# The grouped-query projection ahead of the first scores, and a bias table stored in reverse

## The chip, the cores and the metric

The kernel runs on one core of a Trainium2 chip. The metric is the device time of one execution in microseconds (us). The kernel before takes 1292.56 us, the median of three runs (1289.69 to 1295.23).

The engines are TensorE (PE: matmuls and transposes; PEld is its weight load), VectorE (DVE), ScalarE (ACT), GpSimd (POOL) and SyncE (SP), whose queue issues nearly all transfers.

## The reference

Two post-norm layers on 512 tokens of width 1024. Each layer projects x once, gives the columns to three kinds of attention, joins the heads by one output projection, and ends in a SwiGLU feed-forward part.

```python
for l in range(DEPTH):                       # DEPTH = 2, B = 1, S = 512
    h = x @ w_in[l]                          # 1024 -> 2080 columns
    # A, columns 0 to 415: latent attention (q rank 256, kv rank 128, rotary key 32), 6 heads
    cq, ckv = rms_norm(h[..., :256], mla_q_norm[l]), rms_norm(h[..., 256:384], mla_kv_norm[l])
    ...
    out_a = dense_attention(qa, ka, va, 96 ** -0.5)
    # B, columns 416 to 1567: dilated windows (128,1), (512,4), (2048,16), 6 heads, relative bias
    out_b = dilated_mixture(hb[:, :, 0], hb[:, :, 1], hb[:, :, 2], rel_bias)
    # C, columns 1568 to 2079: grouped-query attention, 4 query and 2 key-value heads
    qc, kc = rms_norm(qc, gqa_q_norm[l]), rms_norm(kc, gqa_k_norm[l])
    qc, kc = (concat([rope(a[..., :32], row_pos), rope(a[..., 32:], col_pos)]) for a in (qc, kc))
    out_c = dense_attention(qc, kc, vc, 64 ** -0.5)
    x = layer_norm(ALPHA * x + concat([out_a, out_b, out_c]) @ w_out[l], ln1_g[l], ln1_b[l])
    ff = (silu(x @ w_gate[l]) * (x @ w_up[l])) @ w_down[l]
    x = layer_norm(ALPHA * x + ff, ln2_g[l], ln2_b[l])
```

All of it is fp32.

## The kernel before

**Precision.** A float32 product is made of three matmuls on split operands: high by high, high by low, low by high (`mm3`, lines 165 to 167). So every weight block is loaded into a staging buffer (`wraw`, line 150, a ring of two), its high part is cast on ScalarE (`whi`, line 152) and its low part subtracted on VectorE or GpSimd (`wlo`, line 156); the table `LOE` names the engine for each kind of weight.

**A layer's projections.** `token_proj` projects columns to tokens: four blocks of 128 tokens (t), each summed over eight blocks of 128 inputs. It serves the value columns of B (96 matmuls of 384 columns, evacuated by `evac_v` into `dv`, line 366), the columns of C (96 matmuls of 512 columns, called the grouped projection here) and the columns of A (96 of 416). `dil_qk(pair)` projects queries and keys of two heads of B (48 matmuls of 512 columns, `qkp`); a pair's keys are copied to the other half of the partitions by transfers (`dk`, line 565). `evac_g2` finishes a token block of the grouped projection: copy, split of the values (`gv`), squares on ScalarE, their sum on VectorE (line 426), the power for the root mean square on GpSimd (line 192), two scalings on VectorE (429, 430, the second by the gain table `gg`), four rotary products on GpSimd (436) and three more operations on VectorE (439 to 446).

**Scores.** `attend` walks over 64 units per layer; a unit is one head's scores for 128 queries: 24 of B, then 16 of C, then 24 of A. Method `a` makes the scores (`sc`, line 241) and the softmax numerators; for B a reduction on VectorE (line 247) adds the bias tile `dt` and finds the extreme in one instruction. Three units later `b` transposes the probabilities (`ptr`, line 264) and splits them (271, 272), and one unit later `c` multiplies them by the values (`po`, 282 and 283).

**Fillers.** Other work is woven between the units as generators: the remaining pairs, the grouped projection, the columns of A, the latents, and the first half of the output projection (`opp`, five of eight blocks). The table `W` gives each filler the first and the last unit between which its steps are spread; `pre` places its weight loads. Before the first unit stand only the value projection, the bias tables and pair zero.

**Order.** Every engine runs its own queue in order. The code's order is the start; the framework's scheduler, which estimates when operands are ready, decides how instructions from neighbouring steps stand against each other in each queue. Within SyncE's queue a transfer waits for those ahead of it to be issued.

**Bias tables (layer 0 only).** `bias_tables` builds a 6 x 1024 table of bias by distance (`nl`: a one-hot matmul `pb` added to the window counts, line 379). Query p of a unit needs the table shifted by p. The table is written to DRAM (`tdr`, 24 KB), spread there to 128 rows of 1025 numbers per head (`skew`, line 385: six transfers of 512 KB) and read back with a row length of 1024, so that each partition starts one number further on (`load_dt`, line 636, 128 x 896). Its matmul takes a bank of the same ring (`ps_mm`) as the value projection and pair zero.

**Gain table.** One buffer `gg` holds C's norm gains of a layer; the loads of layer 1's gains (line 410) reuse it, and VectorE scales them (line 411).

Of the kernel before, what the change touches and what calls it, by code (L numbers as in the profile page):

```python
# [10 lines left out]
F32 = mybir.dt.float32  # L11
# [5 lines left out]
P = 128  # L17
T = 512
# [11 lines left out]
MLA_SCALE = 96.0 ** -0.5  # L30
BRANCHES = ((128, 1), (512, 4), (2048, 16))
NMIX, LA, LC = 13, 3, 1
W = dict(qk1=(3, 4), g2a=(1, 18), qk2=(9, 16), g2b=(10, 16), gT0=(24, 25), gT1=(25, 26), g1=(14, 23), lat=(24, 38),
         lqv=(32, 40), mT=(36, 39, 42, 47, 53, 55), op=(51, 65), tl=69, fl=76, p=(0, 5, 16, 13, 25, 57))
LOE = dict(dl='v', g2='g', op='v', f='g', qk='v', G='g', L='v', uq='v', kv='v', opp='g', rt='g')
QKR = 'wwm'
LEAD = 2
NU = (68, 75)
SPLIT = True
# [3 lines left out]
C_Q, C_K, C_V, C_G = 416, 800, 1184, 1568  # L43
# [13 lines left out]
def _constants():  # L57
    t = np.arange(T)
    rc, rs = _rope_tab(t // GRID_W, HD // 2)
    cc, cs = _rope_tab(t % GRID_W, HD // 2)  # L60
    mc, ms = _rope_tab(t, 32)
    tabs = np.concatenate(
        [np.eye(P), _tok(np.concatenate([rc, cc], 1)), _tok(np.concatenate([rs, cs], 1)), _tok(mc), _tok(ms)], 1
    ).astype(np.float32)
    d = np.arange(-T, T)
    n = np.abs(d)
    nb = BUCKETS // 2
    ex = nb // 2
    nf = np.maximum(n, 1).astype(np.float32)
    large = ex + (np.log(nf / np.float32(ex)) / np.float32(math.log(MAX_DIST / ex)) * np.float32(nb - ex)).astype(np.int32)  # L70
    bucket = np.where(d > 0, nb, 0) + np.where(n < ex, n, np.minimum(large, nb - 1))
    onehot = np.zeros((BUCKETS, 2 * T), np.float32)
    onehot[bucket, np.arange(2 * T)] = -1.0
    cnt = np.zeros(2 * T, np.int64)
    for window, dil in BRANCHES:
        cnt += (d % dil == 0) & (n // dil <= window // (2 * dil))
    neg = np.where(cnt > 0, -np.log(np.maximum(cnt, 1)), 1e30).astype(np.float32)
    return tabs, onehot, neg[None, :]


@with_exitstack
def encoder(ctx: ExitStack, tc, x, w_in, mla_q_norm, mla_kv_norm, w_uq, w_ukv, gqa_q_norm, gqa_k_norm, rel_bias,
            w_out, ln1_g, ln1_b, w_gate, w_up, w_down, ln2_g, ln2_b, tabs, onehot, neglnc, out):
    nc = tc.nc
    V, A, G, TE = nc.vector, nc.scalar, nc.gpsimd, nc.tensor
# [145 lines left out]
    class Head:  # L231
# [4 lines left out]
        def a(self, qt):  # L236

            sc = bank(ps_sc, "sc")
            ops = self.qk(qt)
            for i, (a, b) in enumerate(ops):  # L240
                TE.matmul(sc, a, b, start=i == 0, stop=i == len(ops) - 1)  # L241
            pl = ppl.tile([P, T], F32, tag="l", name="pl")
            nm = small(1, "nm")
            src = sc
            if self.dtile is not None:
                o = 384 - P * qt
                V.tensor_tensor_reduce(out=pl, in0=sc, in1=self.dtile()[:, o:o + T], scale=1.0, scalar=3e38,
                                       op0=ALU.add, op1=ALU.min, accum_out=nm)
                src = pl
            else:  # L250
                V.tensor_reduce(nm, sc, axis=AX.X, op=ALU.min)
            s = small(1, "ssum")
            A.activation(pl, src, AF.Exp, bias=nm, scale=-1.0, accum_out=s)
            r = small(1, "srec")
            V.reciprocal(r, s)  # L255
            G.tensor_tensor(pl, pl, r.to_broadcast([P, T]), op=ALU.mult)  # L256
            self.pl[qt] = pl
# [101 lines left out]
    def run(gen):  # L359
        for _ in gen:  # L360
            pass
# [6 lines left out]
    def bias_tables():  # L368
# [9 lines left out]
            TE.matmul(pb[:6, :], rb, oh[:, i * 512:(i + 1) * 512], start=True, stop=True)  # L378
            V.tensor_tensor(nl[:, i * 512:(i + 1) * 512], nl[:, i * 512:(i + 1) * 512], pb[:6, :], op=ALU.add)
        tdr = dr.tile([6, 2 * T], F32, tag="tdr", name="tdr")  # L380
        nc.sync.dma_start(tdr, nl)

        skew = dr.tile([6, P, 2 * T + 1], F32, tag="skew", name="skew")
        for h in range(6):
            nc.sync.dma_start(skew[h, :, 0:2 * T], tdr[h:h + 1, :].to_broadcast([P, 2 * T]))
        return skew


    skew = []
# [7 lines left out]
    for l in range(DEPTH):  # L397
# [234 lines left out]

        def load_dt(h):
            dt = pdt.tile([P, 896], F32, tag="d", name="dt")
            src = skew[0][h].rearrange("p c -> (p c)")[P:P + P * 2 * T].rearrange("(p c) -> p c", p=P)
            nc.sync.dma_start(dt, src[:, :896])
            dts[h] = dt
            yield

# [39 lines left out]
        if l:  # L679
            run(token_proj(xT, l, C_V, C_G, evac_v, LO["g2"], LATE, ws0))  # L680
        else:
            run(token_proj(xT, l, C_V, C_G, evac_v, V, STAIR, ws0, [ps_mm, ps_mm, ps_sc, ps_sc]))
            skew.append(bias_tables())
        run(dil_qk(0))
        run(load_dt(0))
        run(load_dt(1))
        g2_steps = token_proj(xT, l, C_G, 2080, evac_g2, LO['G'])
        qk = [dil_qk(1), dil_qk(2)]
        g1_steps = token_proj(xT, l, 0, C_Q, evac_g1, LO['L'])
        lqv, op = latent_qv(), out_part()  # L690

        def pre(g, k):
            return (g, 1, W['p'][k], W['p'][k] + 1)

        fillers = [pre(qk[0], 0), (qk[0], 8, *W['qk1']), pre(g2_steps, 1), (g2_steps, 8, *W['g2a']),
                   pre(qk[1], 2), (qk[1], 8, *W['qk2']), (g2_steps, 8, *W['g2b']),
                   (gqa_T(0), 2, *W['gT0']), (gqa_T(1), 2, *W['gT1']), pre(g1_steps, 3), (g1_steps, 16, *W['g1']),
                   (latents(), 4, *W['lat']), pre(lqv, 4), (lqv, 12, *W['lqv'])]
        fillers += [(load_dt(h), 1, 4 * h - 2, 4 * h - 1) for h in range(2, 6)]
# [161 lines left out]
```

## Time and profile before

| what | value |
|---|---|
| median of three runs | 1292.56 us |
| the profiled execution | 1289.81 us |
| its span in the trace | 1288.0 us |
| mean granted TensorE clock | 0.992 |
| TensorE busy | 1252.6 us (97%) |
| six skew writes | 512 KB each |

The span runs from the first to the last recorded instruction; the execution's own time is 1.8 us longer. A granted clock of 1.0 is TensorE at 2.4 GHz, 0.5 at 1.2 GHz; a mean between them is a mixture. The busy time of TensorE is high by nature in this kernel, so the rows to look for are those in which TensorE waits, and the stretches in which another engine sets its pace.

### The profile page before, as it was taken

The page shows a single profiled execution, that of the slowest core. Times are in us where ns is not written, and L with a number is a line of the kernel's source. Part 1 is how long each engine was busy: PE and PEld are TensorE (multiplying, and loading weights), DVE is VectorE, ACT ScalarE, POOL GpSimd, SP SyncE. Part 2 cuts the span into 40 slices and gives each one's busy share as a digit, 9 for nine tenths or more (in the row PEclk, how much of TensorE's full clock was granted, in tenths as well). Part 3 has the DMA queues.
Part 4 walks back from the last instruction along what each step waited for, and adds up shares of the span by engine and source line. Part 5 has one row for each costly group of instructions (what it writes and reads, how often), then busy time and mean ns, then how long its engine had stood idle before and what let it go on. Part 6 is the DMA issues. An engine that isn't in the chain of part 4 may idle for free.

```text
span 1288.0 us, 16749 instructions
## 1 busy us (share of the span) xinstructions
PE 1252.6 (97%) x6352; PEld 1065.2 (83%) x6352; DVE 688.0 (53%) x1138; ACT 543.1 (42%) x955; POOL 323.2 (25%) x344
## 2 busy tenths in 40 slices
PE   8799899999999999999999999999999999999997
PEld 7689788879888888888898898888988888888885
DVE  4259798686333233333564789976843333333346
ACT  3256697554222212222245668865342221122222
POOL 0165474563000000000154456645600000000004
PEclk9999899999999999999999999999999999999999
DMA  5752310323333333333426231105243332333232
GB/s 178 204 137 79 99 40 13 102 83 110 103 96 94 94 96 97 98 98 99 144 80 163 70 99 51 38 14 147 82 114 99 98 98 89 108 96 96 92 100 108
DMA packets 141416, 125.72 MB, mean 98 GB/s; under 512 B 7020, under 2 KB 114668, under 8 KB 141336
## 3 DMA queue, kind: packets, MB, share of 16 engines
q1 hardware_dynamic: 141336, 124.66, 33.1%
q8 instruction: 50, 0.82, 0.3%
q14 instruction: 30, 0.25, 0.1%
HBM read 117.80 MB, written 5.27 MB: 96 GB/s over the span
## 4 chain that ended last, share of the span: by engine, by line
PE 84%; DVE 6%; DMA 4%; ACT 3%; POOL 2%; issue 1%; DVEq 0%; SPq 0%; POOLq 0%; ACTq 0%
PE down L167 6%; PE gate L165 6%; PE down L165 6%; PE up L167 6%; PE up L165 6%; PE down L166 6%; PE gate L167 6%; PE up L166 6%; PE gate L166 6%; PE sc L241 4%; PE ptr L264 3%; PE tp L165 2%; PE tp L166 2%; PE tp L167 2%; PE po L283 2%; PE po L282 2%
## 5 line engine op out<-in xcount | busy, mean ns | idle before, releaser
L152 ACT CAST whi<-wraw 128x1024 fp32r<-128x1024 f32 (+3 forms) x202 | 205.7, 1020 | 553.5 <-PE gate L166 141.8
L156 DVE TENSOR_TENSOR wlo<-wraw,whi 128x1024 fp32r<-128x1024 f32 (+3 forms) x170 | 208.9, 1230 | 319.2 <-ACT whi L152 315.0
L191 POOL TENSOR_TENSOR rstd<-mv,eps_l 128x1 f32<-128x1 f32 x16 | 5.7, 357 | 680.0 <-DVE mv L200 680.0
L256 POOL TENSOR_TENSOR pl<-pl,srec 128x512 f32<-128x512 f32 x128 | 134.2, 1049 | 148.9 <-DVE srec L255 137.4
L166 PE MATMUL gate<-xTl,whi 128*128 128x512 f32 (+1 forms) x384 | 142.9, 372 | 0.0
L166 PE MATMUL up<-xTl,whi 128*128 128x512 f32 (+1 forms) x384 | 142.9, 372 | 0.0
L167 PE MATMUL gate<-xTh,wlo 128*128 128x512 f32 (+1 forms) x384 | 142.8, 372 | 0.0
L167 PE MATMUL up<-xTh,wlo 128*128 128x512 f32 (+1 forms) x384 | 142.8, 372 | 0.0
L165 PE MATMUL up<-xTh,whi 128*128 128x512 f32 (+1 forms) x384 | 142.8, 372 | 0.0
L165 PE MATMUL gate<-xTh,whi 128*128 128x512 f32 (+1 forms) x384 | 142.5, 372 | 0.0
L167 PE MATMUL down<-whi,act 128*128 128x512 f32 x352 | 136.8, 390 | 0.0
L165 PE MATMUL down<-whi,act 128*128 128x512 f32 x352 | 136.8, 390 | 0.0
L166 PE MATMUL down<-wlo,act 128*128 128x512 f32 x352 | 136.8, 390 | 0.0
L156 POOL TENSOR_TENSOR wlo<-wraw,whi 128x512 fp32r<-128x512 f32 (+2 forms) x64 | 79.4, 1263 | 93.4 <-ACT whi L152 72.9
L775 DVE TENSOR_TENSOR sg<-sg,up 128x512 f32<-128x512 f32 x44 | 30.2, 687 | 135.1 <-PE up L167 133.7
L272 DVE TENSOR_TENSOR PTl<-ptr,PTh 128x512 fp32r<-128x512 f32 x128 | 87.2, 682 | 7.8 <-ACT PTh L271 6.8
L271 ACT CAST PTh<-ptr 128x512 fp32r<-128x512 f32 x128 | 75.0, 586 | 38.0 <-PE ptr L264 37.4
L167 PEld LDWEIGHTS gate<-xTh,wlo 128*128 128x128 f32 x384 | 72.4, 189 | 12.5
L166 PEld LDWEIGHTS up<-xTl,whi 128*128 128x128 f32 x384 | 72.4, 189 | 12.5
L165 PEld LDWEIGHTS up<-xTh,whi 128*128 128x128 f32 x384 | 72.4, 188 | 12.5
L167 PEld LDWEIGHTS up<-xTh,wlo 128*128 128x128 f32 x384 | 72.3, 188 | 12.4
L166 PEld LDWEIGHTS gate<-xTl,whi 128*128 128x128 f32 x384 | 72.3, 188 | 12.5
(174 smaller groups left out, 2499.1 us busy)
## 6 DMA issues: line engine op xcount, KB each, us to landing
wraw<-in_ffn_w_down SPq DMA_DIRECT2D x54, 512.0 KB, 3.7
wraw<-in_ffn_w_up SPq DMA_DIRECT2D x44, 512.0 KB, 3.9
wraw<-in_ffn_w_gate SPq DMA_DIRECT2D x44, 512.0 KB, 4.0
wraw<-in_w_in SPq DMA_DIRECT2D x20, 512.0 KB, 4.5
wraw<-in_w_out SPq DMA_DIRECT2D x14, 512.0 KB, 4.0
dt<-skew SPq DMA_DIRECT2D x12, 448.0 KB, 3.2
wraw<-in_w_in SPq DMA_DIRECT2D x8, 416.0 KB, 3.3
wraw<-in_w_in SPq DMA_DIRECT2D x8, 384.0 KB, 3.7
```

What stands on the lines that cost most here:

```text
L152: A.copy(h[:, :n], r[:, :n])
L156: lo.tensor_tensor(o[:, c:c + step], r[:, c:c + step], h[:, c:c + step].bitcast(F32), op=ALU.subtract)
L165: TE.matmul(ps, ah, bh, start=first, stop=False)
L166: TE.matmul(ps, ah, bl, start=False, stop=False)
L167: TE.matmul(ps, al, bh, start=False, stop=last)
L241: TE.matmul(sc, a, b, start=i == 0, stop=i == len(ops) - 1)
L256: G.tensor_tensor(pl, pl, r.to_broadcast([P, T]), op=ALU.mult)
L264: TE.transpose(pb[:, kt * P:(kt + 1) * P], pl[:, kt * P:(kt + 1) * P], ident)
L271: A.copy(ph[:, :, c:c + P], pb)
L272: V.tensor_tensor(plo[:, :, c:c + P], pb, ph[:, :, c:c + P].bitcast(F32), op=ALU.subtract)
L282: TE.matmul(po[:, h0:h0 + 256], self.vst(kt), ph[:, kt], start=kt == 0, stop=False)
L775: V.tensor_tensor(sg, sg, pss[1], op=ALU.mult)
```

## The change

Three edits. The bias table is stored in reverse, so a partition's row is a stretch of the 24 KB table that starts p numbers further on; it is read straight from `tdr` with overlapping rows, `skew` and its six writes go, and the reduction on line 247 reads its tile backwards. The write of `tdr` moves from SyncE's queue to ScalarE's. The grouped projection with its evacuations moves ahead of the first unit in both layers: pair zero's loads, the bias tables (layer 0), the grouped weights' loads, pair zero's matmuls, two bias tiles, then the whole grouped projection. Its low parts move from GpSimd to VectorE (`G`), pair zero's split weights move to the ring `pmix` (`QKR`), and the other fillers get new places in `W`.

```diff
-W = dict(qk1=(3, 4), g2a=(1, 18), qk2=(9, 16), g2b=(10, 16), gT0=(24, 25), gT1=(25, 26), g1=(14, 23), lat=(24, 38),
...
+W = dict(qk1=(1, 7), qk2=(8, 15), gT0=(20, 22), gT1=(28, 30), g1=(13, 25), lat=(25, 30),
...
-LOE = dict(dl='v', g2='g', op='v', f='g', qk='v', G='g', L='v', uq='v', kv='v', opp='g', rt='g')
-QKR = 'wwm'
+LOE = dict(dl='v', g2='g', op='v', f='g', qk='v', G='v', L='v', uq='v', kv='v', opp='g', rt='g')
+QKR = 'mwm'
...
-    onehot[bucket, np.arange(2 * T)] = -1.0
+    onehot[bucket, np.arange(2 * T)[::-1]] = -1.0
...
-    return tabs, onehot, neg[None, :]
+    return tabs, onehot, np.ascontiguousarray(neg[None, ::-1])
...
-                o = 384 - P * qt
-                V.tensor_tensor_reduce(out=pl, in0=sc, in1=self.dtile()[:, o:o + T], scale=1.0, scalar=3e38,
+                o = 895 - (384 - P * qt)
+                V.tensor_tensor_reduce(out=pl, in0=sc, in1=self.dtile()[:, slice(o, o - T if o >= T else None, -1)], scale=1.0, scalar=3e38,
                                        op0=ALU.add, op1=ALU.min, accum_out=nm)
...
         tdr = dr.tile([6, 2 * T], F32, tag="tdr", name="tdr")
-        nc.sync.dma_start(tdr, nl)
-
-        skew = dr.tile([6, P, 2 * T + 1], F32, tag="skew", name="skew")
-        for h in range(6):
-            nc.sync.dma_start(skew[h, :, 0:2 * T], tdr[h:h + 1, :].to_broadcast([P, 2 * T]))
-        return skew
+        A.dma_start(tdr, nl)
+        return tdr
...
-            src = skew[0][h].rearrange("p c -> (p c)")[P:P + P * 2 * T].rearrange("(p c) -> p c", p=P)
-            nc.sync.dma_start(dt, src[:, :896])
+
+            row = skew[0][h:h + 1, :]
+            nc.sync.dma_start(dt, bass.AP(row.tensor, row.offset, [[1, P], [1, 896]]))
...
+        qk = [dil_qk(i) for i in range(3)]
+        g2_steps = token_proj(xT, l, C_G, 2080, evac_g2, LO['G'])
+        next(qk[0])
+        if l == 0:
             skew.append(bias_tables())
-        run(dil_qk(0))
+        next(g2_steps)
+        run(qk[0])
         run(load_dt(0))
         run(load_dt(1))
-        g2_steps = token_proj(xT, l, C_G, 2080, evac_g2, LO['G'])
-        qk = [dil_qk(1), dil_qk(2)]
+
+        run(g2_steps)
...
-        fillers = [pre(qk[0], 0), (qk[0], 8, *W['qk1']), pre(g2_steps, 1), (g2_steps, 8, *W['g2a']),
-                   pre(qk[1], 2), (qk[1], 8, *W['qk2']), (g2_steps, 8, *W['g2b']),
+        fillers = [pre(qk[1], 0), (qk[1], 8, *W['qk1']), pre(qk[2], 2), (qk[2], 8, *W['qk2']),
```

The change moves instructions on all queues; three places follow, each in the order before and then in the changed one. A row is one instruction or a run of like ones: its line, its kind, what it writes and reads, its shape.

SyncE's queue in layer 0, from the bias table's inputs (`nl`) to the first copies of pair zero's keys (`dk`), before:

```order
L375 DMA nl<-in_neglnc 6x1024
L150 DMA wraw<-in_w_in 128x8x128 x4
L381 DMA tdr<-nl 6x1024
L385 DMA skew<-tdr 128x1024 x6
L636 DMA dt<-skew 128x896 x2
L150 DMA wraw<-in_w_in 128x2x512 x2
L565 DMA dk<-dk 64x1024 x2
```

And in the changed kernel:

```order
L375 DMA nl<-in_neglnc 6x1024
L150 DMA wraw<-in_w_in 128x8x128 x2
L150 DMA wraw<-in_w_in 128x2x512 x4
L633 DMA dt<-tdr 128x896 x2
L150 DMA wraw<-in_w_in 128x8x128 x2
L561 DMA dk<-dk 64x1024 x2
```

Between the table's inputs and the keys' copy the six skew writes and the table's own write are gone; two more blocks of the grouped projection (128x2x512) and pair one's two blocks (128x8x128) stand there now.

VectorE's queue at the start of layer 0, from the last split of x (`xTl`) over the value evacuations (`dv`) to the two halves of the bias sum (`nl`), before:

```order
L181 TENSOR_TENSOR xTl<-xtr,xTh 128x512 x3
L366 TENSOR_TENSOR dv<-tp,dv 128x6x64 x3
L156 TENSOR_TENSOR wlo<-wraw,whi 128x1024 x2
L366 TENSOR_TENSOR dv<-tp,dv 128x6x64
L379 TENSOR_TENSOR nl<-nl,pb 6x512 x2
L156 TENSOR_TENSOR wlo<-wraw,whi 128x1024 x2
```

And in the changed kernel:

```order
L181 TENSOR_TENSOR xTl<-xtr,xTh 128x512 x2
L156 TENSOR_TENSOR wlo<-wraw,whi 128x1024 x2
L181 TENSOR_TENSOR xTl<-xtr,xTh 128x512
L366 TENSOR_TENSOR dv<-tp,dv 128x6x64 x3
L156 TENSOR_TENSOR wlo<-wraw,whi 128x1024 x2
L366 TENSOR_TENSOR dv<-tp,dv 128x6x64
L379 TENSOR_TENSOR nl<-nl,pb 6x512 x2
L156 TENSOR_TENSOR wlo<-wraw,whi 128x1024 x2
```

Four subtractions of weights stand before the bias sum where there were two: pair zero's two, and two blocks of the grouped projection right before the last value evacuation.

VectorE's queue in layer 0 around the scaling of layer 1's gain table (`gg`, the last row), from the table's last use in layer 0 (the first row) on, before:

```order
L430 TENSOR_TENSOR g_1130<-g_1130,gg 128x384
L272 TENSOR_TENSOR PTl<-ptr,PTh 128x4x128
L247 ISA pl,nm<-sc,dt 128x512
L247 ISA nm 128x1
L290 TENSOR_TENSOR mf<-po,pvt 64x512
L439 TENSOR_TENSOR g_1130<-g_1130,tab 128x384
L255 RECIPROCAL srec<-ssum 128x1
L441 TENSOR_TENSOR rt<-g_1130,rt 128x384
L247 ISA pl,nm<-sc,dt 128x512
L247 ISA nm 128x1
L446 TENSOR_TENSOR g_1130<-rt,g_1130 128x4x64
L411 TENSOR_SCALAR gg<-gg 128x256
```

And in the changed kernel:

```order
L426 TENSOR_TENSOR g_625<-g_625,gg 128x384
L247 ISA pl,nm<-sc,dt 128x512
L247 ISA nm 128x1
L553 SCALAR_TENSOR_TENSOR dqk<-qkp,dqk 64x512
L435 TENSOR_TENSOR g_625<-g_625,tab 128x384
L255 RECIPROCAL srec<-ssum 128x1
L247 ISA pl,nm<-sc,dt 128x512
L247 ISA nm 128x1
L437 TENSOR_TENSOR rt<-g_625,rt 128x384
L553 SCALAR_TENSOR_TENSOR dqk<-qkp,dqk 64x512
L407 TENSOR_SCALAR gg<-gg 128x256
```

The scaling stood at the end of the last grouped evacuation, among late units of B; it now stands behind the first two units' reductions and the two evacuations of pair one's queries (`dqk`).

## Rows read from the trace of the kernel before

**Rows 1.** The page: busy time, share of the span and instructions of each engine.
```profile
PE 1252.6 (97%) x6352; PEld 1065.2 (83%) x6352; DVE 688.0 (53%) x1138; ACT 543.1 (42%) x955; POOL 323.2 (25%) x344
```
**Rows 2.** Windows of units 0-15, 16-23, 24-39 in both layers: PE, PEld, DVE, ACT, POOL, PEclk, DMA.
```profile
61.46:125.80 64.34, 63.85 (x330) 54.63 (x331) 47.30 (x103) 40.51 (x83) 39.54 (x48) 0.97 0.39 107
125.80:157.40 31.60, 25.98 (x140) 23.15 (x138) 24.12 (x62) 19.76 (x52) 15.19 (x20) 0.90 0.31 92
157.40:193.50 36.10, 34.66 (x248) 31.46 (x247) 33.48 (x67) 31.51 (x73) 25.37 (x26) 1.00 0.16 45
693.60:757.30 63.70, 63.65 (x340) 54.86 (x339) 48.30 (x104) 40.78 (x84) 34.92 (x44) 1.00 0.36 96
757.30:782.80 25.50, 22.60 (x138) 20.71 (x138) 23.25 (x59) 18.69 (x50) 14.90 (x18) 0.99 0.35 107
782.80:819.50 36.70, 35.64 (x248) 32.63 (x247) 33.92 (x67) 32.34 (x76) 25.38 (x26) 0.96 0.15 43
```
**Rows 3.** Timeline, layer 0, bias sum and pair zero: start, duration, engine, line, operation.
```profile
31.76 0.67 DVE L379 TENSOR_TENSOR nl<-nl,pb 6x512 f32<-6x512 f32 x1
...
32.57 0.47 PE L165 MATMUL qkp<-xTh,whi 128*128 128x512 f32 x1
```
**Rows 4.** Timeline of PE, layer 1: pair zero's first matmul, the first scores.
```profile
673.76 0.39 PE L165 MATMUL qkp<-xTh,whi 128*128 128x512 f32 x1
...
693.63 0.62 PE L241 MATMUL sc<-dk,dqk 128*128 128x512 f32 x2
```
**Rows 5.** Timeline of PE, layer 0: last projection matmul and first scores.
```profile
54.21 0.39 PE L167 MATMUL qkp<-xTh,wlo 128*128 128x512 f32 x1
61.46 0.76 PE L241 MATMUL sc<-dk,dqk 128*128 128x512 f32 x1 [6.86 <-DMA dk<-dk]
```
**Rows 6.** Timeline of SP's queue, layer 0: the skew writes and the keys' copy.
```profile
35.96 4.72 SPq L385 DMA_DIRECT2D skew<-tdr  x6
...
47.34 0.52 SPq L565 DMA_DIRECT2D dk<-dk  x1
```
**Rows 7.** Transfers from 36 to 62 us: size and median time to landing.
```profile
dk<-dk SPq DMA_DIRECT2D x2, 256.0 KB, 12.2
```
**Rows 8.** Windows around two low-clock stretches of layer 0, columns as in rows 2.
```profile
60.00:64.00 4.00, 2.54 (x6) 2.09 (x7) 1.99 (x4) 3.44 (x5) 3.28 (x3) 0.50 0.02 9
64.00:68.00 4.00, 4.00 (x15) 2.97 (x14) 0.76 (x3) 1.29 (x3) 2.70 (x3) 0.81 0.72 176
154.30:157.70 3.40, 3.35 (x15) 3.36 (x16) 2.50 (x6) 1.40 (x3) 0.28 (x1) 0.51 0.30 113
```
**Rows 9.** Timeline of SP and DVE, layer 0: gain table's loads and scaling.
```profile
124.58 1.30 SPq L410 DMA_DIRECT2D gg<-in_gqa_q_norm  x3
...
133.31 0.29 DVE L411 TENSOR_SCALAR gg<-gg 128x256 f32<-128x256 f32 x1 [4.60 <-DMA gg<-in_gqa_q_norm]
```
**Rows 10.** Groups by line: the reduction with bias; busy, mean ns, idle before.
```profile
L247 DVE CUSTOM_DVE_ANT_0 pl<-sc,dt 128x512 f32<-128x512 f32 x48 | 32.7, 682 | 6.1 <-PE sc L241 5.0 <-ACT sq L472 0.3 <-POOL pl L256 0.3
```
**Rows 11.** Start of layer 0: pair-zero load's issue, value evacuation; casts and landing, 15-40.
```profile
21.33 0.39 SPq L150 DMA_DIRECT2D wraw<-in_w_in  x1
...
31.29 0.56 DVE L366 TENSOR_TENSOR dv<-tp,dv 128x384 fp32r<-128x384 f32 x1 [0.19 <-ACT dv L365]
...
L152 ACT CAST whi<-wraw x6: 837/1052/1056, 15.6 to 36.1; 128x1024 fp32r<-128x1024 f32 x4, 128x768 fp32r<-128x768 f32 x2
...
DMA to landing us min/median/max: 3.8/4.3/4.9
```
**Rows 12.** Line 156 on DVE, 60 to 130 us: ns minimum/median/maximum, starts, forms.
```profile
L156 DVE TENSOR_TENSOR wlo<-wraw,whi x6: 1019/1236/2111, 85.6 to 114.7; 128x832 fp32r<-128x832 f32 x4, 128x1024 fp32r<-128x1024 f32 x2
```
**Rows 13.** Timeline of PE, layer 0: a wait for split probabilities.
```profile
154.35 0.58 PE L283 MATMUL po<-PTl,dv 128*128 128x256 f32 x1 [2.31 <-DVE PTl L272]
```
**Rows 14.** Timeline of POOL in one grouped evacuation: power and four rotary products.
```profile
92.31 1.34 POOL L192 TENSOR_TENSOR rstd<-rstd,mhalf 128x6 f32<-128x6 f32 x1
94.91 1.45 POOL L436 TENSOR_TENSOR rt<-g,tab 128x96 f32<-128x96 f32 x4 [1.26 <-DVE g L430]
```

More of the change, by code (lines that the diff above doesn't have):

```diff
@@ L32 @@
 NMIX, LA, LC = 13, 3, 1
-W = dict(qk1=(3, 4), g2a=(1, 18), qk2=(9, 16), g2b=(10, 16), gT0=(24, 25), gT1=(25, 26), g1=(14, 23), lat=(24, 38),
-         lqv=(32, 40), mT=(36, 39, 42, 47, 53, 55), op=(51, 65), tl=69, fl=76, p=(0, 5, 16, 13, 25, 57))
-LOE = dict(dl='v', g2='g', op='v', f='g', qk='v', G='g', L='v', uq='v', kv='v', opp='g', rt='g')
-QKR = 'wwm'
+W = dict(qk1=(1, 7), qk2=(8, 15), gT0=(20, 22), gT1=(28, 30), g1=(13, 25), lat=(25, 30),
+         lqv=(30, 40), mT=(36, 39, 42, 47, 53, 55), op=(46, 65), tl=69, fl=76, p=(0, 5, 5, 10, 25, 44))
+LOE = dict(dl='v', g2='g', op='v', f='g', qk='v', G='v', L='v', uq='v', kv='v', opp='g', rt='g')
+QKR = 'mwm'
 LEAD = 2
```

## The prediction, made before the change was run

> **What bounds the kernel now.** I read the busy shares first: TensorE is busy 1252.6 of 1288.0 us [rows 1]. The change keeps its matmuls to the column, so only its waits can go. Next I cut the two attention stages into stretches of score units (a unit is one head's scores for 128 queries; 64 per layer), the busy time of each engine in each. In layer 1, units 0 to 15 take 63.70 us with TensorE busy 63.65: TensorE sets the pace. Units 16 to 39 take 25.50 + 36.70 = 62.2 us with VectorE busy 57.2 of them: there VectorE sets it. The same stretches of layer 0 take 64.34, 31.60 and 36.10 [rows 2]. From the first projection matmul of pair zero (32.57 in layer 0, 673.76 in layer 1 [rows 3, 4]) to unit 40 (193.5 and 819.5) layer 0 needs 160.9 us and layer 1 145.7, for the same work. The change can reach these 15.2 us.
>
> **Where layer 0 loses them.** The largest wait of TensorE is the first score matmul's, 6.86 us for the copied keys: it ran out of matmuls at 54.21 and went on at 61.46, though the pair-one projection had already been pulled in front [rows 5]. The keys' copy was issued from 47.34 on, behind the six 512 KB writes of the skewed table (35.96 on), and such copies took 12.2 us to land in that stretch [rows 6, 7]. Then TensorE's clock was granted at 0.50 (1.2 GHz instead of 2.4) from 60 to 64 and at 0.81 on average from 64 to 68 [rows 8]: with what it did after 61.46 some 4.0 us at the lower level, so 2 us lost. The second loss: layer 1's gain table cannot be loaded before layer 0's last use of it; its loads are issued from 124.58 on, and VectorE, which has the scaling of that table in its queue, stands idle 4.60 us until 133.31 [rows 9]. Layer 1 has no such load, and its units 16 to 23 take 25.5 instead of 31.6 [rows 2]: 6.1 us. Together 7 + 2 + 6 = 15 of the 15.2.
>
> **The change, part by part.** *Table.* Six writes of 512 KB and the reads for them go; the head tables, 448 KB as before, are read straight from the 24 KB table. Between it and the keys' copy the queue now holds four weight blocks of 512 KB for the grouped projection and two of pair one. Even at the 12.2 us of the crowded stretch the copy, ready at about 47 + 3.5 (the 3.5 is worked out below), lands by 63; the 96 moved matmuls keep TensorE until 70. So this wait goes, at no price. The reversed read: 48 reductions, 682 ns each now [rows 10]. The trace shows none; bounds: 0.68, as now (fewer elements it does not read), and a second pass, 2 x 0.68 = 1.36. I take 0.68, the same instruction on the same shapes. The second pass would cost nothing in units 0 to 15 of the new order (VectorE 48 of 49 us there, by the paragraph on the order) and 8 x 0.68 = 5.4 us in units 16 to 23 of each layer, 10.9 in all.
>
> *Gain table.* In the new order seven instructions stand between the table's last use and the scaling, where now there are eight, but among them is a pair-one evacuation that must wait for 24 matmuls of 0.23 us behind the first scores: 5.5 us. The loads have that time to land, and TensorE has 45 projection matmuls (10.2 us) beside it. The 4.60 us are covered; uncovered, they cost 6.1 again.
>
> *Start of layer 0: a new wait.* The bias sum (nl) frees the bank for the first projection. Now its first half ends at 32.43 and TensorE goes on at 32.57 [rows 3]. In the new order two subtractions of grouped-projection weights stand before it, and their casts on ScalarE stand before the last value evacuation. With two staging buffers the second of these loads can be issued only when the second pair-zero block has been subtracted: that block is issued at 21.33 + 0.39, lands a median 4.3 us later, is cast (1.05) and subtracted (1.24) by 28.2 [rows 11, 12]. A load takes 3.8 to 4.9, median 4.3, so the second grouped one lands at 32.5; its cast 1.05, subtraction 1.24, the value evacuation 0.56 [rows 11, 12] and the bias sum 0.67 end at 36.0. TensorE stands 3.5 us (3.0 to 4.1 by the bounds of the load; 0 if the load came four microseconds early). After a wait of this size it falls to the lower level: behind the 2.31 us wait that ends at 154.35 the granted clock is 0.51 from 154.3 to 157.7 [rows 8, 13]. So another 3.4/2 = 1.7, together 5.2. The Trainium skill (TensorE: Matmul & The Clock Gate, What's actually happening) has the throttled state as the one the array falls back to when idle, released by activity; the trace agrees (0.51 behind the 2.31 us wait), and by it the new hole is paid twice, as here.
>
> *Order.* The grouped projection (96 matmuls) now stands before the first score and pair one (48) behind it. A matmul of 512 columns takes (693.63 - 673.76)/87 = 0.228 us [rows 4]. Before the first score there are 144 matmuls instead of 96 in layer 0 and 87 in layer 1. Layer 0: 32.57 + 5.2 + 144 x 0.228 = 70.6 instead of 61.5: +9.1. Layer 1: 57 x 0.228 = +13.0; it has no bias sum there, so no hole.
> Units 0 to 15 lose 57 matmuls of 512 columns net (13.0 us) and 8 transpositions and 11 value matmuls, of half that width at most (19 x 0.114 = 2.2), and gain 3 of 416 columns (0.6): 63.7 - 14.6 = 49.1, still TensorE's pace, for VectorE has 80 instructions there instead of 105: 48.30 x 80/105 = 36.8 us [rows 2], and 16 x 0.68 = 10.9 more with the second pass. Layer 1: -14.6; layer 0: 49.1 - 64.3 = -15.2.
> Units 16 to 39, at VectorE's pace, keep their count: 131 instructions instead of 129. 62.2 x 131/129 = 63.2; I take 64.0, since the value matmuls left over from before come in. Bounds: 57.2 x 131/129 = 58.1 if VectorE never waits; 72 with two more holes of 2.3 + 1.7. Layer 1: +1.8; layer 0: 64.0 - 67.7 = -3.7.
> From unit 40 on eight output matmuls of 512 columns come earlier, out of the stretch that TensorE sets into one with slack: -0.9 in each layer.
>
> *Sum.* Layer 0: 9.1 - 15.2 - 3.7 - 0.9 = -10.7. Layer 1: 13.0 - 14.6 + 1.8 - 0.9 = -0.7. Together -11.4. Everything behind attention is untouched. The profiled execution took 1289.81 us (span 1288.0), which gives 1278.4; the median of the three runs, 1292.56, lies 2.75 above it and would give 1281.2. I put the forecast between them, at 1280.
>
> **Rivals.**
> *Units 16 to 39 starve (slower).* The projections that fed TensorE while VectorE worked are used up earlier, and from unit 16 on TensorE waits for probabilities. For it: the wait that ends at 154.35 [rows 13] comes from that stretch. Against it: it holds nearly the same work before and after. Price: a hole of that size with its low clock is 2.3 + 1.7 = 4.0; three more per layer make 24: 1304. It decides from about one and a half more per layer.
> *VectorE comes late to the first units; layer 1 gives the gain back.* The four grouped evacuations now run packed into 22 us (96 x 0.228) beside GpSimd's part of them: a power of 1.34 and four rotary products of together 1.45 per token [rows 14], 11.2 us. If all of it delays VectorE, the 10.2 us cover of the pair-one matmuls is used up, and a hole of 2.3 + 1.7 falls on each layer: 8 us back, 1288. The Trainium skill (SBUF — State Buffer, Who interferes with whom) has VectorE's second port pair shared with GpSimd under an exclusive lock, which speaks for this rival; no run here shows it yet.
> *Smoother than thought.* VectorE fills its waits in units 16 to 39 (58.1 instead of 64.0 in both layers): 1268.
> *The keys come late all the same*, behind the weight blocks in the same queue: the 7 us stay, 1287. Against it: some 16 us of matmuls after the copy is ready.
>
> **How the numbers follow.** Forecast 0.56 (1273 to 1287), smoother 0.13, given back (by a late VectorE, or by the second pass, which gives 1291) 0.18, late keys 0.06, starving 0.07. About 0.5% (6.5 us) can be told from no change, so faster means under 1286.1 and slower above 1299.0. Faster: nearly all of the forecast, all of smoother, a small part of given back: 0.71. Slower: most of starving, 0.06. Within 0.5%: 0.23. The range, 1268 to 1291, leaves out starving and the ends of smoother and of given back.
>
> **What would show it.** Right: no wait of the first score matmul for the copied keys; first scores at about 70 and 707 us; no low clock in layer 0 but one near 36 to 40; a TensorE wait of 3 to 4 us before the first projection matmul of pair zero, ended by the bias sum; no VectorE wait for the gain table; units 16 to 39 at 64 us in both layers. Wrong: a reduction over 0.75 us, low clock in units 16 to 39 of both layers, or a first score waiting for VectorE. If layer 1 moves by more than 5 us either way, the term for units 16 to 39 failed.

## The result and the profile after

The changed kernel takes 1301.0 us, the median of four runs (1299.38 to 1301.94), against 1292.2 for the kernel before beside it: a ratio of 1.0066, 95% interval 1.0042 to 1.0090. It is slower; the forecast was 1280. The profiled executions stand the same way: spans of 1297.6 and 1288.0 us.

TensorE is as busy as before, and VectorE's busy time, reversed read included, has not moved. The page's busy line and, from the groups by line, the reduction:

```profile
PE 1255.1 (97%) x6352; PEld 1061.2 (82%) x6352; DVE 688.0 (53%) x1146; ACT 543.0 (42%) x955; POOL 304.4 (23%) x328
```
```profile
L247 DVE CUSTOM_DVE_ANT_0 pl<-sc,dt 128x512 f32<-128x512 f32 x48 | 32.7, 681 | 13.4 <-PE ptr L264 8.2 <-POOL pl L256 4.2 <-PE sc L241 0.5
```

A reduction takes 681 ns against 682 [rows 10]: reading the tile backwards costs nothing.

The windows of units 0 to 15, 16 to 23 and 24 to 39, layer 0 and then layer 1, answer to [rows 2] (columns as there):

```profile
71.91:125.30 53.39, 49.39 (x267) 42.53 (x266) 40.34 (x91) 33.59 (x70) 21.95 (x27) 1.00 0.42 116
125.30:150.10 24.80, 23.51 (x152) 21.80 (x151) 17.95 (x48) 17.79 (x44) 12.62 (x14) 1.00 0.25 81
150.10:191.80 41.70, 38.01 (x260) 32.49 (x258) 36.41 (x82) 34.56 (x84) 29.26 (x32) 1.00 0.17 51
711.60:762.40 50.80, 49.28 (x267) 42.53 (x266) 40.29 (x90) 35.02 (x71) 21.95 (x27) 1.00 0.43 116
762.40:787.50 25.10, 23.75 (x152) 21.80 (x151) 17.94 (x48) 17.78 (x43) 12.57 (x14) 1.00 0.26 83
787.50:830.20 42.70, 39.45 (x259) 33.93 (x258) 36.52 (x82) 34.63 (x84) 29.24 (x32) 0.96 0.18 50
```

In both layers units 24 to 39 are 5.5 to 6 us longer than before (36.1 and 36.7). VectorE has no more to do in units 16 to 39 as a whole: 57.2 us in layer 1 before, 54.5 now. But its share in units 24 to 39 rose from 33.9 to 36.5 us, and in units 16 to 23 it is now idle for 7 of 25 us and TensorE sets the pace. TensorE's longest waits in units 24 to 39 of layer 1 are two transposes of the latents that wait for VectorE's work on them (the view lists who waited for whom: us in total, times, longest); layer 0 has the same two:

```profile
PE lt L484 <- DVE lat L488: 1.0, 1, 1.0
PE lt L484 <- DVE g L470: 0.7, 1, 0.7
```

The timeline of PE answers to [rows 3 to 5]: first projection matmul of pair zero and first score in layer 0, a wait at the second unit's transposes (`ptr`), and the same two starts in layer 1.

```profile
36.34 0.80 PE L165 MATMUL qkp<-xTh,whi 128*128 128x512 f32 x1 [2.62 <-DVE nl L379]
...
71.91 0.62 PE L241 MATMUL sc<-dk,dqk 128*128 128x512 f32 x2
...
87.69 0.55 PE L264 MATMUL ptr<-tab,pl 128*128 128x128 f32 x3 [2.48 <-POOL pl L256]
...
678.82 0.50 PE L165 MATMUL qkp<-xTh,whi 128*128 128x512 f32 x1 [0.75 <-DVE dv L366]
...
711.58 0.61 PE L241 MATMUL sc<-dk,dqk 128*128 128x512 f32 x2
```

The first score no longer waits for the copied keys. Pair zero of layer 0 starts at 36.34 instead of 32.57, close to the 36.0 worked out, though TensorE's wait is 2.62 us and not 3 to 4. That it comes so close is in part luck: in the other profiles with the changed order of layer 0's start (e1, e2, e3, e6, e8, e10, e11) it starts between 34.7 and 36.3, behind waits of 2.5 to 3.2 us. Layer 1's start was thought free: from its first value-projection matmul to pair zero it now takes 22.7 us instead of 18.9. And VectorE stands still for the gain table, as before [rows 9]; its timeline at the start and behind the first scores, and GpSimd's scaling of the second unit's probabilities:

```profile
34.01 1.23 DVE L156 TENSOR_TENSOR wlo<-wraw,whi 128x1024 fp32r<-128x1024 f32 x1 [1.66 <-ACT whi L152]
35.15 0.55 DVE L366 TENSOR_TENSOR dv<-tp,dv 128x384 fp32r<-128x384 f32 x1
35.62 1.26 DVE L379 TENSOR_TENSOR nl<-nl,pb 6x512 f32<-6x512 f32 x2
...
86.05 0.29 DVE L407 TENSOR_SCALAR gg<-gg 128x256 f32<-128x256 f32 x1 [3.37 <-DMA gg<-in_gqa_q_norm]
86.26 0.15 DVE L255 RECIPROCAL srec<-ssum 128x1 f32<-128x1 f32 x1
...
86.50 1.14 POOL L256 TENSOR_TENSOR pl<-pl,srec 128x512 f32<-128x512 f32 x1 [4.94 <-DVE srec L255]
```

The granted clock behind the start hole, and TensorE's busy time behind the gain table (windows):

```profile
36.30:40.00 3.70, 3.66 (x9) 2.90 (x10) 1.81 (x2) 1.96 (x2) 0.00 (x0) 0.50 0.45 145
40.00:44.00 4.00, 4.00 (x14) 3.20 (x13) 1.23 (x1) 0.03 (x1) 0.00 (x0) 0.71 0.87 263
...
84.00:88.00 4.00, 1.51 (x11) 1.11 (x10) 1.92 (x6) 1.01 (x2) 1.14 (x1) 1.00 0.10 23
```

After the 2.62 us wait TensorE ran at 1.2 GHz from 36.3 to 40 and partly so to 44: 3.7 x 0.5 + 4.0 x 0.29 = 3.0 us lost, where 1.7 was reckoned. Other profiles of the same start lost less (last section).

### The profile page after: what moved, and what is told of

Same layout as the page of the kernel before. It is cut to its first block, busy times and chain, and to the rows that moved or that the text cites. A ratio compares the mean times of both kernels' runs of the same rounds, so it can differ in the third digit from the quotient of the medians.

```text
span 1297.6 us, 16740 instructions
## 1 busy us (share of the span) xinstructions
PE 1255.1 (97%) x6352; PEld 1061.2 (82%) x6352; DVE 688.0 (53%) x1146; ACT 543.0 (42%) x955; POOL 304.4 (23%) x328
## 4 chain that ended last, share of the span: by engine, by line
PE 80%; DVE 7%; DMA 5%; ACT 3%; POOL 3%; issue 2%; SPq 0%; DVEq 0%; POOLq 0%; ACTq 0%
PE gate L165 6%; PE up L165 6%; PE up L167 6%; PE up L166 6%; PE gate L167 6%; PE gate L166 6%; PE down L165 5%; PE down L167 5%; PE down L166 5%; PE sc L241 4%; PE ptr L264 3%; PE tp L165 2%; PE tp L166 2%; PE tp L167 2%; PE po L283 2%; PE po L282 2%
## 5 line engine op out<-in xcount | busy, mean ns | idle before, releaser
L156 DVE TENSOR_TENSOR wlo<-wraw,whi 128x1024 fp32r<-128x1024 f32 (+3 forms) x178 | 217.8, 1224 | 315.7 <-ACT whi L152 310.2
L272 DVE TENSOR_TENSOR PTl<-ptr,PTh 128x512 fp32r<-128x512 f32 x128 | 86.5, 683 | 14.4 <-ACT PTh L271 13.7
L271 ACT CAST PTh<-ptr 128x512 fp32r<-128x512 f32 x128 | 74.2, 586 | 28.1 <-PE ptr L264 26.7
L165 PEld LDWEIGHTS gate<-xTh,whi 128*128 128x128 f32 x384 | 72.3, 188 | 12.5
```

Source lines behind the costliest of these rows:

```text
L156: lo.tensor_tensor(o[:, c:c + step], r[:, c:c + step], h[:, c:c + step].bitcast(F32), op=ALU.subtract)
L165: TE.matmul(ps, ah, bh, start=first, stop=False)
L271: A.copy(ph[:, :, c:c + P], pb)
L272: V.tensor_tensor(plo[:, :, c:c + P], pb, ph[:, :, c:c + P].bitcast(F32), op=ALU.subtract)
```

## The experiments

Two tables hold what the traces gave: us from pair zero's first projection matmul to the first score, then the stretches between the first scores of units 0, 16, 24 and 40, then to the first feed-forward matmul. That last end shifts with the queue's order: in layer 0 the first feed-forward matmul stands about 2.2 us before the last matmul of the output projection in the kernel before, the changed kernel, e4, e7 and e9, and behind it in e1, e8, e10, e11 and e12; in layer 1 it stands behind it in all but e1 (4.7 us before). A trace is one execution: that of e1 is the longest of its five (1314.48 us), that of e10 the shortest of its six (1296.88).

| layer 1 | to score | 0-15 | 16-23 | 24-39 | 40 on | sum |
|---|---|---|---|---|---|---|
| before | 19.9 | 63.7 | 25.5 | 36.7 | 97.2 | 243.0 |
| changed | 32.8 | 50.8 | 25.1 | 42.7 | 96.2 | 247.6 |
| e1_old_fillers | 32.8 | 50.8 | 31.9 | 36.4 | 101.7 | 253.6 |
| e8_latents_early | 32.8 | 58.1 | 23.8 | 39.5 | 95.1 | 249.3 |
| e10_a_columns_23 | 32.8 | 50.8 | 29.6 | 39.1 | 96.0 | 248.3 |
| e11_latents_38 | 32.8 | 50.8 | 25.3 | 41.8 | 96.1 | 246.8 |
| e9_holes_mended | 32.8 | 50.8 | 24.7 | 42.2 | 96.1 | 246.6 |
| e12_mended_latents | 32.7 | 50.8 | 24.6 | 40.4 | 96.4 | 244.9 |
| e7_table_gain | 20.3 | 63.7 | 26.7 | 36.6 | 97.2 | 244.5 |

| layer 0 | pair zero at | to score | 0-15 | 16-23 | 24-39 | 40 on |
|---|---|---|---|---|---|---|
| before | 32.6 | 28.9 | 64.4 | 31.5 | 36.2 | 95.0 |
| changed | 36.3 | 35.6 | 53.4 | 24.8 | 41.7 | 98.0 |
| e4_table_only | 32.1 | 19.9 | 63.8 | 31.8 | 36.2 | 94.8 |
| e9_holes_mended | 31.6 | 32.9 | 50.7 | 25.1 | 41.7 | 96.4 |
| e12_mended_latents | 31.6 | 32.8 | 50.7 | 24.7 | 41.8 | 99.1 |
| e7_table_gain | 32.1 | 20.1 | 63.9 | 25.6 | 36.7 | 95.8 |

Ratios are to the kernel before on the same chip.

**e4_table_only and e5_order_only: the two edits apart.** The kernel before with the table's hunks of the change, and the changed kernel with those hunks undone:

```diff
 # e4: the kernel before
-            nc.sync.dma_start(skew[h, :, 0:2 * T], tdr[h:h + 1, :].to_broadcast([P, 2 * T]))
+        A.dma_start(tdr, nl)
...
 # e5: the changed kernel
+            nc.sync.dma_start(skew[h, :, 0:2 * T], tdr[h:h + 1, :].to_broadcast([P, 2 * T]))
-        A.dma_start(tdr, nl)
```

> The kernel before with the reversed table alone (no skew, tiles read straight from the 24 KB table, reversed read on VectorE, table written from ScalarE's queue); W, LOE, QKR and the place of the grouped projection as before. Theory: the copied keys are no longer late, the 6.86 us wait of the first score and some 2 us at the lower clock go: 1292 - 8 = 1284, units 16 to 23 keep their wait for the gain table. Rival, keys late all the same behind the weight blocks: no change, 1292. A cost of the reversed read would show as reductions over 0.70 us.

> The changed kernel with the table of before (skew written and read, normal read on VectorE, table written from SyncE's queue); the order, W, LOE and QKR as changed. With the kernel before and the table alone (0.992 of before) it completes the square of the two edits. Theory: the two edits take away the same wait, since 96 projection matmuls cover the copied keys whether the skew writes are there or not; then order alone is within 3 us of the changed kernel, about 1.007 of before, and the table is worth 10 us by itself but nearly nothing behind the new order. Rival, the effects add: order alone is 10 us slower than the changed kernel, 1.014 of before, and the order costs 18 us whatever the table.

The table alone: 1280.91 us, ratio 0.9924 (0.9912 to 0.9937). The order alone: 1299.59, ratio 1.0072 (1.0058 to 1.0087); both: 1.0066. Behind the new order the table is worth nothing that can be measured, by itself it is worth 9.8 us. In the table alone the first score comes at 51.98, with no wait ahead of it, and copies of the keys land in 4.2 us instead of 12.2 [rows 7]:

```profile
51.98 0.47 PE L241 MATMUL sc<-dk,dqk 128*128 128x512 f32 x1
```
```profile
dk<-dk SPq DMA_DIRECT2D x3, 256.0 KB, 4.2
```

So the forecast's largest gain is real, and it belongs to the table; the new order takes the same wait away by covering it, and costs 1.0066 - 0.9924 = 1.4%, 18 us, beside it.

**e6_layer1_old_order: where the order costs.** `run(g2_steps)` only in layer 0; layer 1 has the fillers, `W`, ring and engine of before.

```diff
-        run(g2_steps)
+        W = WL[l]
+        if l == 0:
+            run(g2_steps)
...
+        if l:
+            fillers += [pre(g2_steps, 1), (g2_steps, 8, *W['g2a'])]
```

> The changed kernel in layer 0; in layer 1 the grouped projection goes back among the fillers, with the table W, the ring and the engine of the low parts of before. Theory: the order costs layer 1 about 8.5 us (3.7 at its start, 5 between unit 24 and the feed-forward part), so about 1.000 of before. Rival, the loss of layer 1 is carried over from layer 0 or lies in what both orders share: under 2 us gained.

1291.15 us, 1.0007 (0.9997 to 1.0018). Layer 1 accounts for 0.6%, some 7.6 us, the rest of the 18 is layer 0's.

**e2_pair0_ring: layer 1's start.**

```diff
-... LO['qk'], QKR[pair]) for c in (C_Q, C_K)]
+... LO['qk'], 'w' if l and pair == 0 else QKR[pair]) for c in (C_Q, C_K)]
```

> The changed kernel with pair zero's split weights of layer 1 alone back in the ring wh/wl (QKR 'w' there). Theory, queue at the start of layer 1: the free ring let pair zero's casts and subtractions slip in front of the last splits of x and layer-norm steps on ScalarE and VectorE (the cast waited 2.5 us for its load at 654.6); back in the small ring they stand behind, and the first projection matmul of layer 1 comes 3.7 us earlier after the end of layer 0: about 1297. Rival, the grouped weights: the start is late because four grouped blocks and pair zero share two staging buffers, whatever the ring; no change, or a loss of up to 3 us where the grouped blocks now wait for the ring (first score of layer 1 not earlier).

1294.76 us, 1.0031 (1.0018 to 1.0043): 0.35% or 4.5 us less than the changed kernel. The way from layer 1's first value-projection matmul to pair zero is 18.9 us again, as before. ScalarE's timeline in the changed kernel has the mechanism: pair zero's two casts (128x1024) wait for their loads, the first for 1.54 us and the second for 2.49, with splits of x (`xTh`) behind each. The second cast of the x2 row is one of a value block.

```profile
649.19 1.05 ACT L152 CAST whi<-wraw 128x1024 fp32r<-128x1024 f32 x1 [1.54 <-DMA wraw<-in_w_in]
...
654.62 1.78 ACT L152 CAST whi<-wraw 128x1024 fp32r<-128x1024 f32 x2 [2.49 <-DMA wraw<-in_w_in]
656.31 0.58 ACT L180 CAST xTh<-xtr 128x512 fp32r<-128x512 f32 x1
```

The small ring had kept them out, since the value blocks held its buffers: in the kernel before the same two casts stand at 670.89, after a wait for a value matmul.

**e3_gain_late: the gain table.**

```diff
+        if l:
+            V.tensor_copy(gg[0:1, 0, 0:1], xt[0:1, 0, 0:1])
         for i in range(6):
```

> The changed kernel with one more 1-element copy on VectorE that ties layer 1's first gain load to the first token block of layer 0's output, so that neither this load nor the scaling of the table can stand in layer 0's queue. Theory, gain table: VectorE's 3.37 us wait for that load at 86 us holds up the third unit's reduction and the pair-one keys; TensorE is busy only 1.5 of 4 us from 84 to 88. Without it units 0 to 15 of layer 0 take what they take in layer 1, 50.8 instead of 53.4 us: about 1298.3. Rival, VectorE and GpSimd are late there anyway from the packed grouped evacuations: under 1 us, and the wait is replaced by another one on the third unit's probabilities.

1296.09 us, 1.0044 (1.0029 to 1.0059): 2.8 us less. Units 0 to 15 of layer 0 take what they take in layer 1:

```profile
69.40:120.10 50.70, 49.20 (x268) 42.57 (x266) 40.28 (x90) 33.62 (x70) 21.94 (x27) 1.00 0.44 121
```

VectorE's order from the first score to unit 39 is otherwise the same, so the 2.7 us (53.4 to 50.7) were that wait.

**e1_old_fillers, e8_latents_early, e10_a_columns_23, e11_latents_38: units 24 to 39.** The changed kernel with other entries of `W`:

```diff
-W = dict(... gT0=(20, 22), gT1=(28, 30), g1=(13, 25), lat=(25, 30), lqv=(30, 40), ... p=(0, 5, 5, 10, 25, 44))
+e1:      ... gT0=(24, 25), gT1=(25, 26), g1=(14, 23), lat=(24, 38), lqv=(32, 40), ... p=(0, 5, 5, 13, 25, 44))
+e8:      ... g1=(8, 20), lat=(20, 30), lqv=(28, 40), ... p=(0, 5, 5, 6, 22, 44))
+e10:     ... g1=(13, 23)
+e11:     ... lat=(24, 38)
```

> The changed kernel with the table W of before for the two key transposes of C (gT0, gT1), the columns of A (g1), the latents (lat) and their projections (lqv); everything else as changed. Theory, fillers: units 24 to 39 take 41.7 and 42.7 us in the changed kernel instead of 36.1 and 36.7 because the latents' evacuations, the late columns of A and a transpose are packed into units 24 to 30, where VectorE is then the bound, and the matmuls of lqv are left over for units 31 to 39. Spread as before, both stretches come back to about 37 us: some 10 us less, 1291. Rival, left-over work: the evacuations moved ahead of the scores push value matmuls into these units whatever W says; then both stretches stay above 40 us and the time within 2 us of 1301. In between if units 16 to 23 take over the loss.

> The changed kernel with the columns of A in units 8 to 19 (13 to 24 now), the latents in 20 to 29 (25 to 29) and their projections in 28 to 39 (30 to 39), weight loads with them. Theory: in units 0 to 23 TensorE sets the pace and VectorE is idle for some 17 us per layer (busy 40.3 of 50.8 and 17.9 of 25.1 us in layer 1), from unit 24 on VectorE is the bound for a stretch; evacuations moved from the second part to the first shorten units 24 to 39 from 42 to about 38 us in both layers and cost the first part as many us as it gets matmuls: net 4 to 8 us less, 1.001 to 1.004 of before. Rival, transfer of the wait: what leaves units 24 to 39 starves another stretch, as with the fillers of before: no gain or a loss, 1.006 to 1.012.

> The changed kernel with one entry of W: the columns of A end two units earlier (g1 13 to 23 instead of 13 to 25, as before). Theory, left-over scalings: 2.2 us of the scalings of A's columns (3.3 us of VectorE in units 24 to 31 against 1.1 before) delay the latents, and with them the uq projections (3.5 us of TensorE in units 24 to 31 against 7.2), which then pile up in units 32 to 39; with g1 over by unit 23 both halves shrink to about 19 us, while units 13 to 22 get longer by what moves there: net 4 to 8 us less over both layers, 1.001 to 1.004 of before. Rival, the latents' own entry (25 to 30): under 2 us.

> The changed kernel with one other entry of W: the latents in units 24 to 37 instead of 25 to 29, as before. Theory, left-over scalings of A's columns: they still hold up the latents, so units 24 to 39 stay above 40 us: within 2 us of the changed kernel, 1.006. Rival, the latents' packing: the last transposes and the rotary key leave units 24 to 31 and units 24 to 39 come down by 3 us or more per layer, 1.001 or less.

They took 1307.92 us (1.0145, 1.0122 to 1.0169), 1298.27 (1.0068, 1.0056 to 1.0081), 1301.39 (1.0082, 1.0066 to 1.0098) and 1293.23 (1.0017, 1.0008 to 1.0026). The stretch did what the theory of e1 said, the time did not. With the old entries units 24 to 39 are at 36.4 us again, but units 16 to 23 take 6.8 us more and those from 40 on 5.5 more:

```profile
766.90:798.80 31.90, 27.41 (x163) 23.98 (x161) 22.17 (x57) 19.10 (x50) 14.54 (x18) 0.95 0.27 81
798.80:835.10 36.30, 34.70 (x231) 29.53 (x231) 31.96 (x68) 31.98 (x74) 25.06 (x26) 1.00 0.14 41
835.10:936.80 101.70, 96.58 (x527) 80.09 (x527) 71.89 (x140) 58.14 (x119) 53.11 (x50) 0.97 0.23 64
```

e8 moves the loss into units 0 to 15, as its rival had it. In e10 units 24 to 39 come down to 39.1 in both layers, as its theory had it, but units 16 to 23 take 4.5 to 4.8 us more, and the gain does not come. e11's run gained 6 us by the ratio and 8.2 by the spans, but layer 1's stretches only 0.8 and layer 0's units 24 to 39 only 1.3; another 2.6 are its earlier first score (69.3 instead of 71.9, with the same instructions up to there: the start scatters between profiles, 71.0 in e1 and 69.4 to 69.6 in e3, e8 and e10). A further 2.7 lie in layer 0 between unit 40 and the first matmul on the feed-forward tile `down` (234.5 us in the changed kernel, 231.7 in e11), which the table's shifting end hides. Its theory, no gain, fell; how much of the gain is the entry's is for e12 to say.

What the unevenness is, the halves of units 24 to 39 in layer 1 show. The windows of the kernel before, and below them the first half's work on the tile uq alone (the projections of the latents):

```profile
782.80:800.90 18.10, 17.85 (x124) 16.49 (x123) 16.76 (x36) 15.52 (x37) 9.78 (x10) 0.92 0.10 29
800.90:819.50 18.60, 17.79 (x126) 16.15 (x125) 17.16 (x32) 16.82 (x39) 15.60 (x17) 1.00 0.21 57
```
```profile
782.80:800.90 18.10, 3.79 (x24) 3.40 (x24) 1.23 (x3) 0.92 0.10 29
```

The same two views of the changed kernel:

```profile
787.50:808.50 21.00, 18.29 (x116) 15.30 (x115) 19.86 (x48) 16.60 (x42) 12.19 (x15) 0.92 0.18 51
808.50:830.20 21.70, 21.17 (x145) 18.63 (x144) 16.66 (x35) 18.03 (x42) 17.05 (x18) 1.00 0.18 50
```
```profile
787.50:808.50 21.00, 1.57 (x12) 1.63 (x12) 0.40 (x1) 0.92 0.18 51
```

Before, both halves are even, VectorE busy 16.8 and 17.2 us. Now VectorE has 19.9 of 21.0 us to do in the first half, with 12 uq matmuls for TensorE instead of 24, and in the second half TensorE sets the pace with what was left (145 matmuls, 126 before). Neither engine can lend its idle time to the other half. This account is read from the tables and in part argued: the runs with other entries show that the stretch can be shortened, e12 below that more even halves come with a shorter stretch (18 and 30 uq matmuls, 20.8 and 19.7 us, in layer 1), but none evens the halves and leaves the stretches beside them alone.

**e9_holes_mended, e12_mended_latents, e7_table_gain: what is left.**

```diff
 # e9: the changed kernel, with the copy of e3
-QKR = 'mwm'
+QKR = 'wwm'
 # e12: e9, with
-lat=(25, 30)
+lat=(24, 38)
 # e7: e4, with the copy of e3
```

> The changed kernel with pair zero's split weights in the small ring in both layers (QKR 'wwm' as before), which puts the bias sum of layer 0 ahead of the grouped blocks again, and with the copy that takes the gain table out of layer 0's queue. Theory, a sum of places: layer 0's start gives back 3.7 us and about 1.8 of low clock, layer 1's start 3.7, the gain table 2.7: 12 us off the changed kernel's 1.0066, so 0.998 of before; units 24 to 39 stay at 42 us in both layers, which is the 8 to 10 us that then still separate it from the table alone with the same copy (0.990). Rival: the places overlap, or grouped blocks that come later starve the grouped projection: 1.002 or more.

> The mended kernel (QKR 'wwm', the gain table's copy) with the latents in units 24 to 37. Theory, independent places: what the latents' entry gave in the changed kernel (1.0066 to 1.0017) comes on top of 0.996, so 0.991 to 0.993 of before, level with the table alone and the same copy (0.990). Rival, most of that gain was the spread of the start between runs (first score at 69.3 instead of 71.9 us, with the same instructions) and units 24 to 39 give 1 to 3 us in all: 0.994 to 0.996, and the order of before stays better by 4 us or more.

> The table alone, with the 1-element copy that takes the gain table's load and scaling out of layer 0's queue; order as before. Theory: the gain table's wait (4.60 us of VectorE at 133 in the kernel before, with 6.1 us longer units 16 to 23 than in layer 1) goes as well: 0.992 - 0.004 = 0.988 of before, 1275. Rival: VectorE has other work to make up there and the wait was half hidden: 0.991, within 2 us of the table alone.

e9: 1284.86 us, 0.9960 (0.9947 to 0.9972), 13.7 us under the changed kernel by the ratios, where the three places promised 12. Pair zero of layer 0 starts at 31.6. Units 24 to 39 stay long:

```profile
140.40:182.10 41.70, 38.00 (x260) 32.50 (x258) 36.41 (x82) 34.52 (x84) 29.25 (x32) 1.00 0.18 51
772.00:814.30 42.30, 38.15 (x260) 32.58 (x259) 37.13 (x82) 34.68 (x84) 28.88 (x32) 1.00 0.17 50
```

e12: 1280.88, 0.9932 (0.9918 to 0.9945). The latents' entry adds 0.3% or 3.6 us (1.8 by the spans), between its two theories: some of e11's gain was the start. e7: 1276.63, 0.9901 (0.9887 to 0.9914), the fastest kernel of the study, and it has the order of before. The copy is worth 0.23% there, 3.0 us by the ratios and 3.9 by the spans (1278.8 and 1274.9), between its theory (0.988) and its rival (0.991). Its units 16 to 23 of layer 0 are 6.2 us shorter than e4's and now take what they take in layer 1 of the kernel before, but part of that is lost again in later stretches:

```profile
116.00:141.60 25.60, 22.70 (x139) 20.72 (x137) 23.27 (x59) 18.76 (x50) 14.92 (x18) 0.99 0.36 112
```

Between e9 and e7 lie 0.6%, 7.6 us by the ratios and 6.6 by the spans; units 24 to 39 are 5.0 and 5.6 us longer in e9, and the other stretches together 4.0 shorter.

## Why the prediction was wrong

Between the forecast of -11.4 us and the +9.6 of the two spans lie 21 us. Term by term:

| step | forecast | measured | shown by |
|---|---|---|---|
| keys' wait of layer 0 | gone | gone | first score at 71.91 without a wait, e4 |
| reversed read | 0.68 us | 0.681 | [rows 10] and its row above |
| start of layer 0 | 3.5 + 1.7 us | 3.8 + 3.0 (other profiles 2.1 to 3.7, and 1.5 to 2.5 on the way to the first score) | e9, where both are gone |
| start of layer 1 | "no hole" | 3.8 us | e2 |
| gain table | "covered" | 2.7 us | e3 |
| units 16 to 39 | 64.0 us in each layer | 66.5 and 67.8 | e1, e8, e10 |
| units 0 to 15 | 49.1 us | 50.8 without the gain table's wait | e3, layer 1 |
| from unit 40 on | -0.9 us per layer | +3.0 and -1.0 | tables; +1.4 and -1.1 in e9 |

By the traces' stretches, some 6.3 of the 21 us lie in units 16 to 39, 3.8 each from unit 40 on and at the start of layer 1, 3.2 in the size of units 0 to 15, 2.7 in the gain table and 1.4 at the start of layer 0.

The step that failed most is the term for units 16 to 39. It took them as one stretch at VectorE's pace and scaled it by the count of VectorE's instructions, 131 for 129. The 129 is layer 0's count, and the 62.2 us that it scaled are layer 1's, which has 126 [rows 2]; that alone would make 64.7 us. In fact VectorE's busy time there fell, from 57.2 to 54.5 us, and the time rose: units 16 to 23 had come under TensorE's pace, VectorE's idle time there was lost, and its work and TensorE's then stood in different halves of the rest. With [rows 2] alone one could have seen that TensorE was busy for 58.2 of the 62.2 us, no less than VectorE, and that 25.5 us with TensorE busy 22.6 leave little room for 152 matmuls instead of 138. The prediction's own sign for this failure came: layer 1 moved by more than 5 us, by 8.4 from its first value-projection matmul to the feed-forward part, 3.8 of them at its start. The rival of starving units had the place right, at a chance of 0.07, but not its form: in units 24 to 39 there is no wait of 2.3 us, the longest is 1.0 in either layer, and the granted clock is 1.00 in layer 0 and 0.96 in layer 1.

The second failure is of a kind: the order of the queues was read at the start of layer 0 and not at the start of layer 1. The ring that lets pair zero's weights be staged early let them in front of the splits of x there. "It has no bias sum there, so no hole" looked for the same wait instead of the same cause.

The third: the gain table's "cover" counted TensorE's 45 matmuls, and what stood behind the waiting instruction on VectorE was the second unit's reciprocal (`srec`), which GpSimd needs to scale that unit's probabilities. TensorE had its matmuls until about 85 us and then waited, until 87.69, for these probabilities. The loads were issued from 77.88 on; the time to 86.05 is 8.2 us, against the 5.5 us reckoned. The trace of before had this size: 8.7 us from 124.58 to 133.31 [rows 9].

From unit 40 on the sum let output matmuls come earlier for nothing. In layer 0 TensorE waits 4.5 us there, for a split of probabilities, for the split weights of the output projection's first half (`opp`, whose first unit in `W` moved from 51 to 46) and for VectorE's additions in its second half (`op`), against 1.0 before:

```profile
PE po L282 <- ACT PTh L271: 1.5, 1, 1.5
PE op L165 <- DVE xtok L738: 1.2, 2, 0.7
PE opp L166 <- POOL wlo L156: 1.0, 2, 0.9
PE opp L165 <- ACT whi L152: 0.8, 1, 0.8
```

No run takes this place apart, so its cause stays open.

In units 0 to 15 the 49.1 us take TensorE as never idle; without the gain table's wait it is busy 49.2 to 49.3 of 50.7 to 50.8 us. The rival of a late VectorE, at 4 us per layer, did not come there.

Last, the sum counts the end of the keys' wait once, but did not ask which edit ends it. e4 and e5 show one wait and two remedies: the table ends it at no price, and the order, which ends it too, is 18 us dearer.

What stays open: whether some table `W` makes the new order as good as the old one. Four were tried beside the changed one; in layer 1, from pair zero to the feed-forward part, they took 246.8 to 253.6 us, against 243.0 before. With the places of e9 mended, e12 takes 244.9 there and e7 244.5, so most of the 4 us between their times stands in layer 0. The move of the grouped weights' low parts to VectorE was not run apart.

## What to carry to other kernels

When two edits both remove one wait, measure them apart: here the cheap one (the table) was worth 9.8 us, and the expensive one hid that. When work moves out of a stretch, say for each stretch after it which engine sets the pace, since equal totals in uneven halves cost time. And a larger buffer ring is also a change of order: what a ring had held back will stand in front of something, in every layer that uses it.

## Not expected of the hardware

Behind nearly the same wait the granted clock was not low for equally long in every execution. In the changed kernel it was 0.50 from 36.3 to 40.0 and 0.71 to 44.0 behind a wait of 2.62 us, 3.0 us lost; in e3, with the same instructions up to there, it was 0.66 from 35.0 to 40.0 and 1.00 behind that after a wait of 2.54 us, 5.0 x 0.34 = 1.7 us lost, as much as the forecast had from [rows 8, 13]:

```profile
35.00:40.00 5.00, 4.99 (x15) 3.96 (x16) 2.91 (x3) 2.10 (x2) 0.00 (x0) 0.66 0.59 154
40.00:44.00 4.00, 4.00 (x19) 3.30 (x18) 0.78 (x2) 0.84 (x2) 0.00 (x0) 1.00 1.03 309
```

And it fell without a long wait: in layer 1 of the changed kernel TensorE's two waits for the latents (0.7 and 1.0 us) stand just ahead of this stretch, while the same two waits in layer 0 left the clock at 1.00. Units 24 to 39 take 42.7 us in layer 1 and 41.7 in layer 0:

```profile
796.70:800.10 3.40, 3.40 (x15) 3.21 (x16) 3.40 (x7) 3.10 (x7) 1.04 (x1) 0.51 0.00 0
```
